# Output projection of a hybrid attention layer: two 16-bit halves instead of two four-byte halves, and its weights loaded earlier

## The chip, the cores and the metric

One core of one Trainium2 chip runs the whole layer as one program. The metric is the device time of one execution in microseconds; lower is better. Engines are named as in the profile: PE is TensorE (PEld its weight loads), DVE is VectorE, ACT is ScalarE, POOL is GpSimd, SP is SyncE, which issues nearly all DMAs here.

## The reference, cut to what matters

A layer takes 1024 prompt tokens and 8 x 8 sample tokens of width 1024, normalises them, projects them with one wide matrix into queries, keys, values and gates, runs two kinds of attention (a sparse one with a compressed, a selected and a window branch, 8 heads; and a dense one with forget gates, 8 heads, called fox), and merges:

```
def merge_out(x, oa, za, ob, zb, w_out):
    B, T, _ = x.shape
    u = jnp.concatenate([oa.reshape(B, T, -1) * jax.nn.silu(za), ob.reshape(B, T, -1) * jax.nn.silu(zb)], axis=-1)
    return x + jnp.einsum('btm,md->btd', u, w_out).astype(x.dtype)
```

`w_out` is 1024 x 1024 in four-byte floats (4.2 MB). The change concerns this last product, for the prompt (`yp`) and for the samples (`ys`).

## The kernel before, in words

Prompt tokens are worked on in 8 tiles of 128, the 64 sample tokens as a ninth (t = 8, `NT`). The kernel runs in stages that flow into one another.

1. Projections (about 0 to 520 us). Fifteen chunks of columns of the input matrix (`chunks`, L800), each for nine token tiles. Operands are split into a high and a low 16-bit half, and a product is three matmuls: high x high, high x low, low x high (`project`, L240). `load_w` (L181) loads a chunk, squares it on ScalarE for its norm, scales it by the norm and splits it. While chunk ci runs, at its fourth tile, the functions of `background` (L808) for that chunk are called: compression of cached tokens, masks, decay sums. Chunks 5 to 8 are the keys and queries of the fox heads. `x_tile` (L158) loads the tokens at the start into buffers `xin` (5 of them), with squares into `xsq`.
2. Fox attention (about 400 to 595 us), the last projection chunks woven in.
3. Sparse tiles 0 to 3 (L1421, about 580 to 775 us), the samples' attention woven in by `fill` (L954) from `sample_filler` (L1394). A tile (`nsa_tile`, L1378) loads and splits the next tile's keys and queries (L1004, L1018), takes row maxima on VectorE (`nsa_max`, L1036), and per pair of key blocks computes scores on TensorE, the exponential `pf` and its high half `phi` on ScalarE (L1103, L1104), the low half `plo` on VectorE or, in every third case here, on GpSimd (L1106), and three matmuls with the values (`pv`, L719).
4. Sparse tiles 4 to 7 (L1576) and the output projection (L1448 to L1579). Weights: `load_wout` (L1454) loads 128 rows in two halves of 512 columns into `wos` (2 buffers); ScalarE writes the high half `woh` (L1459), GpSimd the low half `wol` (L1460), both as F32R, a four-byte matmul format. `project_out` (L1462) does a tile: load `z` (the gates, parked in DRAM) and `obl` (the fox result), four VectorE products into `z` (L1475), eight transposes (L1485), `uh` on ScalarE (L1487), `ul` on VectorE (L1488), 2 x 24 matmuls of 512 columns (L1499), addition of the input token (L1501). `z`, `uh`, `ul` and `xr` have one buffer each. For the samples high and low halves lie side by side and 2 x 16 matmuls do (L238, called from L1495). `project_last` (L1523) does tile 7 in three parts (fox columns, then two pairs of blocks of the sparse result), accumulating all three into the same two PSUM banks, and adds the token at the end (L1552).

Order of work. The program is written as a sequence; a scheduler that simulates a timeline (L1609) then fixes the order of each engine's instructions ahead of the run, taking later work early where its operands and buffers are free. In the run each engine, and SyncE as issuer of DMAs, goes through its list in order. The output projections stand behind tiles 4 to 7 in the program and are pulled forward between their instructions. On-chip memory of the samples' pools (`S5`) is freed at L1446, and the pools of the output projection are laid there.

## Time and profile before

| what | value |
| --- | --- |
| median of 3 runs | 977.35 us (974.95 to 984.67) |
| profiled execution | 974.53 us |
| its span (first to last instruction) | 972.8 us |
| mean granted TensorE clock in it | 0.988 |
| TensorE busy | 901.1 us (93%) |
| VectorE / ScalarE / GpSimd busy | 644.9 / 612.3 / 397.4 us |
| DMA | 111.73 MB, mean 115 GB/s |

A matmul's duration in the trace (0.39 us for 512 columns) overlaps with its neighbours; the distance between starts is what a stream of them costs. "Busy" of an engine is the union of its instructions.

### The profile page before, as it was taken

To read this page: it belongs to the slowest core of one execution; us is meant where nothing else is said; L and a number is where in the kernel's file an instruction comes from. 1 tells how busy PE (TensorE), PEld (TensorE's weight loads), DVE (VectorE), ACT (ScalarE), POOL (GpSimd) and SP (SyncE) were. 2 spreads that over 40 slices of the span, in tenths; PEclk is the share of its full clock that TensorE was granted. 3 is DMA by queue.
4 is the path that set the end of the run, shared out by engine and by line. 5 is a ranking of instruction groups with operands and counts; after the bars stand their busy time and mean duration, and the time that the engine had idled before them with its cause. 6 is when DMAs were issued, how large, how long until landed. Compare 5 with 4: busy or idle time off the path is not lost.

```text
span 972.8 us, 24636 instructions
## 1 busy us (share of the span) xinstructions
PE 901.1 (93%) x9097; PEld 707.1 (73%) x9097; DVE 644.9 (66%) x1845; ACT 612.3 (63%) x1328; POOL 397.4 (41%) x571
## 2 busy tenths in 40 slices
PE   4898999889999999999998888889999979999997
PEld 3687889878888988878786556656666645776776
DVE  5764666564555426768777566887888989776552
ACT  6844643433454665797786779888897868454540
POOL 4544567754676432342425123434333157211100
PEclk9999999999999999999999899999999999999999
DMA  7563323422343332331314755555355032231241
GB/s 267 142 154 110 90 81 89 107 59 70 98 117 99 117 106 65 106 110 54 88 43 125 234 154 154 164 170 177 114 167 185 5 129 97 97 108 57 76 140 66
DMA packets 119740, 111.73 MB, mean 115 GB/s; under 512 B 37100, under 2 KB 100244, under 8 KB 119596
## 3 DMA queue, kind: packets, MB, share of 16 engines
q1 hardware_dynamic: 117732, 106.74, 36.4%
q0 software_dynamic: 1456, 2.83, 1.3%
q8 instruction: 71, 1.16, 0.5%
q10 hardware_dynamic: 432, 0.59, 0.2%
q14 instruction: 49, 0.40, 0.1%
HBM read 79.57 MB, written 27.41 MB: 110 GB/s over the span
## 4 chain that ended last, share of the span: by engine, by line
PE 64%; DVE 9%; DMA 7%; ACT 6%; issue 3%; POOL 2%; SPq 1%; DVEq 0%; ACTq 0%; POOLq 0%
PE acc L245 22%; PE ctr L1499 7%; PE sa L474 3%; PE acc L238 3%; PE smax L1054 2%; PE pv L726 2%; PE pv L724 2%; PE pv L725 2%; PE st L1098 2%; PE st L1099 2%; DMA wst<-in_w_in_dram 2%; DVE junk L744 2%; PE ctr L1547 1%; PE st L774 1%; PE st L775 1%
## 5 line engine op out<-in xcount | busy, mean ns | idle before, releaser
L245 PE MATMUL acc<-wsp,xth 128*128 128x256 f16 (+1 forms) x1920 | 334.7, 275 | 5.1 <-ACT xth L175 2.6
L245 PE MATMUL acc<-wsp,xtl 128*128 128x256 f16 (+1 forms) x960 | 264.1, 275 | 0.0
L245 PEld LDWEIGHTS <-xth 128*128 128x128 f16 x1920 | 187.3, 99 | 33.7 <-ACT xth L175 3.1
L1103 ACT ACTIVATE pf<-st,nsc 128x512 f32<-128x512 f32 x132 | 99.0, 780 | 49.6 <-PE st L1099 26.9
L245 PEld LDWEIGHTS <-xtl 128*128 128x128 f16 x960 | 94.5, 98 | 14.8 <-issue 1.4
L724 PEld LDWEIGHTS <-phi 128*128 128x128 f16 x816 | 76.9, 97 | 17.0 <-issue 5.5
L726 PEld LDWEIGHTS <-plo 128*128 128x128 f16 x816 | 76.7, 99 | 9.8 <-DVE plo L1106 2.4
L1104 ACT ACTIVATE phi<-pf 128x1024 f16<-128x1024 f32 (+1 forms) x76 | 71.7, 948 | 14.0 <-PE pv L726 8.8
L725 PEld LDWEIGHTS <-phi 128*128 128x128 f16 x816 | 76.8, 97 | 4.7 <-issue 1.5
L1106 DVE TENSOR_TENSOR plo<-pf,phi 128x1024 f16<-128x1024 f32 (+1 forms) x58 | 67.0, 1158 | 10.8 <-ACT phi L1104 10.0
L711 ACT ACTIVATE pf<-st,nsc 128x512 f32<-128x512 f32 (+1 forms) x96 | 62.5, 670 | 16.1 <-PE st L775 5.2
L264 POOL TENSOR_TENSOR nss<-nss,nhalf 128x4 f32<-128x4 f32 (+3 forms) x72 | 68.4, 950 | 4.4
L724 PE MATMUL pv<-va,phi 128*128 128x65 f16 x528 | 59.0, 193 | 4.3 <-DVE nt L1083 3.4
L716 DVE TENSOR_TENSOR plo<-pf,phi 128x512 f16<-128x512 f32 (+3 forms) x77 | 51.6, 674 | 16.0 <-ACT phi L714 15.7
L201 ACT ACTIVATE vsq<-wst 128x512 f16<-128x512 f32 (+2 forms) x72 | 40.2, 559 | 33.4 <-DMA wst<-in_w_in_dram 32.5
L725 PE MATMUL pv<-va,phi 128*128 128x64 f16 x528 | 58.9, 195 | 0.0
L726 PE MATMUL pv<-va,plo 128*128 128x65 f16 x528 | 56.4, 192 | 0.4 <-DVE plo L1106 0.2
L1106 POOL TENSOR_TENSOR plo<-pf,phi 128x1024 f16<-128x1024 f32 (+1 forms) x18 | 34.6, 1923 | 51.4 <-ACT phi L1104 40.6
L714 ACT ACTIVATE phi<-pf 128x512 f16<-128x512 f32 (+1 forms) x96 | 48.7, 524 | 10.3 <-PE pv L726 8.8
L1054 PE MATMUL smax<-kma,nqm 88*128 88x512 f16 (+3 forms) x192 | 49.1, 316 | 3.8 <-DVE nm L744 3.5
L1084 POOL TENSOR_TENSOR oa<-oa,nt 128x256 f32<-128x256 f32 x22 | 19.7, 894 | 78.8 <-DVE nt L1083 65.0
L1098 PE MATMUL st<-nqm,kma 88*128 88x512 f16 x132 | 50.2, 380 | 0.9 <-ACT pf L1103 0.7
(446 smaller groups left out, 2402.6 us busy)
## 6 DMA issues: line engine op xcount, KB each, us to landing
wst<-in_w_in_dram SPq DMA_DIRECT2D x56, 256.0 KB
sfk<-in_cache_fox_kv_dram SPq DMA_DIRECT2D x32, 256.0 KB
sfv<-in_cache_fox_kv_dram SPq DMA_DIRECT2D x32, 256.0 KB
out_dram<-kv SPq DMA_DIRECT2D x52, 128.0 KB
xin<-in_x_prompt_dram SPq DMA_DIRECT2D x8, 512.0 KB
cpair<-in_cache_nsa_cmp_kv_dram SPq DMA_DIRECT2D x64, 64.0 KB
zpark<-z SPq DMA_DIRECT2D x32, 128.0 KB
spg<-in_cache_nsa_slc_kv_dram SPq DMA_DIRECT2D x32, 128.0 KB
```

The costliest lines, as they stand in the source:

```text
L245: nc.tensor.matmul(ps[:, :n], x[:, k, t * 128:(t + 1) * 128], w[k // 2][:, i, k % 2, :n], start=(k == 0 and j == 0), stop=(k == KT - 1 and ...
L264: nc.gpsimd.tensor_tensor(ss[:n, 0, :h], ss[:n, 1, :h], nhalf[:n, :h], op=ALU.pow)
L711: nc.scalar.activation(p[:n, :cols], ps[:n, :cols], AF.Exp, bias=nsc[:n, 3:4], scale=nsc[:n, 6:7])
L724: nc.tensor.matmul(po[:, s, 0:65], hi[:, c], v[:, 0:65], start=f, stop=False, skip_group_check=True)
L725: nc.tensor.matmul(po[:, s, 0:64], hi[:, c], v[:, 65:129], start=False, stop=False, skip_group_check=True)
L726: nc.tensor.matmul(po[:, s, 0:65], lo[:, c], v[:, 0:65], start=False, stop=l, skip_group_check=True)
L1054: nc.tensor.matmul(pr[:, r], qm[0:88, (r0 + r) * 128:(r0 + r + 1) * 128], kma[0:88, 2 * k + g, j0 * 128:j1 * 128], start=r == 0, stop=not ...
L1098: nc.tensor.matmul(ps, kma[0:88, 2 * k + g, c], qm[0:88], start=True, stop=False)
L1103: nc.scalar.activation(pf[:, 512 * x:512 * x + 512], ps, AF.Exp, bias=nsc[:, 3:4], scale=nsc[:, 2:3])
L1104: nc.scalar.activation(hi[:, 0:n], pf[:, 0:n], AF.Copy)
L1106: (nc.gpsimd if turn[0] % share[mixed[0]] == 0 else nc.vector).tensor_sub(lo_[:, 0:n], pf[:, 0:n], hi[:, 0:n])
L1499: nc.tensor.matmul(ps, l[:, k], w[:, k, c], start=(k == 0 and j == 0), stop=(k == KT - 1 and j == 2))
```

## The change

Weights and tokens of the output projection are held as 16-bit halves. So that they fit the 16-bit range, the weights are scaled by one factor from the norm of the whole matrix, each token's row by a factor from its own norm, and the product is scaled back where the input token is added. The matrix's norm is computed during chunks 5 to 9 of the projections (`wout_squares`, `wout_scale`), which loads the matrix once more; the splitting load moves to the start of each of the sparse tiles 0 to 3, two blocks of rows per tile. In `project_last` each of the three parts gets its own scale and its own accumulation, added to `x` in turn; the last part uses the score banks.

```
+    wsc = P.tile([128, 16], F32, name="wsc")
...
+    def wout_squares(ks):
+        for k in ks:
+            s = B.tile([128, D], F32, name="xin", bufs=5)
+            nc.sync.dma_start(s, w_out[:, k])
+            junk = B.tile([128, D], F32, name="xsq")
+            nc.scalar.activation(junk, s, AF.Square, accum_out=wsc[:, k:k + 1])
+    def wout_scale():
+        p = PS.tile([128, 8], F32, name="sa", bufs=1)
+        nc.tensor.matmul(p, ones, wsc[:, 0:8], start=True, stop=True)
+        nc.vector.tensor_reduce(out=wsc[:, 10:11], in_=p, axis=AX.X, op=ALU.add)
+        nc.vector.tensor_scalar(wsc[:, 11:12], wsc[:, 10:11], 2.0 ** -30, TINY, op0=ALU.mult, op1=ALU.add)
+        nc.gpsimd.tensor_tensor(wsc[:, 8:9], wsc[:, 11:12], nhalf[:, 0:1], op=ALU.pow)
+        nc.vector.reciprocal(wsc[:, 9:10], wsc[:, 8:9])
...
-                  4: [lambda: cmp_cached(2)], 5: [lambda: cmp_cached(3)], 6: [sample_compressed, lambda: score_scales()],
-                  7: [setup_masks, finish_gates], 8: [fox_decay, load_logf], 9: [fox_first]}
+                  4: [lambda: cmp_cached(2)], 5: [lambda: cmp_cached(3), lambda: wout_squares((0, 1))],
+                  6: [sample_compressed, lambda: score_scales(), lambda: wout_squares((2, 3))],
+                  7: [setup_masks, finish_gates, lambda: wout_squares((4, 5))],
+                  8: [fox_decay, load_logf, lambda: wout_squares((6, 7))], 9: [fox_first, wout_scale]}
...
+    W3 = S3.enter_context(tc.tile_pool(name="wout", bufs=1, reuse_waits="tile"))
+    woh = W3.tile([128, KT, D], F16, name="woh")
+    wol = W3.tile([128, KT, D], F16, name="wol")
+    def load_wout(k):
+        for h in range(2):
+            c = slice(512 * h, 512 * h + 512)
+            st = W3.tile([128, 512], F32, name="wos", bufs=2)
+            nc.sync.dma_start(st, w_out[:, k, c])
+            nc.scalar.activation(st, st, AF.Copy, scale=wsc[:, 8:9])
+            nc.scalar.activation(woh[:, k, c], st, AF.Copy)
+            nc.gpsimd.tensor_sub(wol[:, k, c], st, woh[:, k, c])
     mixed[0] = 1
     for t in range(4):
+        for k in (2 * t, 2 * t + 1):
+            load_wout(k)
         qq = nsa_tile(t, qq)
...
+    def token_scale(u, n):
+        w = u.shape[-1]
+        junk = B6.tile([128, D], F16, name="uj", bufs=1)
+        s = B6.tile([128, 4], F32, name="us", bufs=4)
+        nc.scalar.activation(junk[:n, 0:w], u, AF.Square, accum_out=s[:n, 0:1])
+        nc.gpsimd.tensor_scalar(s[:n, 1:2], s[:n, 0:1], 2.0 ** -30, TINY, op0=ALU.mult, op1=ALU.add)
+        nc.gpsimd.tensor_tensor(s[:n, 2:3], s[:n, 1:2], nhalf[:n, 0:1], op=ALU.pow)
+        nc.scalar.activation(u, u, AF.Copy, scale=s[:n, 2:3])
+        nc.vector.reciprocal(s[:n, 3:4], s[:n, 2:3])
+        nc.vector.tensor_tensor(s[:n, 0:1], s[:n, 3:4], wsc[:n, 9:10], op=ALU.mult)
+        return s[:n, 0:1]
...
+        undo = token_scale(u[:n], n)
-        uh = B6.tile([128, KT, 128], F32R, name="uh", bufs=1)
+        uh = B6.tile([128, KT, 128], F16, name="uh", bufs=1)
...
-            nc.vector.tensor_tensor(x[:n, c], ps[:n], x[:n, c], op=ALU.add)
+            nc.vector.scalar_tensor_tensor(x[:n, c], ps[:n], undo, x[:n, c], op0=ALU.mult, op1=ALU.add)
...
+        for ks, src, early in ((slice(4, 8), obl, True), (slice(0, 2), nsa[:, 0:256], True), (slice(2, 4), nsa[:, 256:512], False)):
...
+            undo = token_scale(u, 128)
...
+                ps = PS.tile([128, 512], F32, name="ctr", bufs=CTR) if early else PM.tile([128, 512], F32, name="st", bufs=2)
...
+                nc.vector.scalar_tensor_tensor(x[:, c], ps, undo, x[:, c], op0=ALU.mult, op1=ALU.add)
+                if not early:
+                    nc.sync.dma_start(o["yp"][0, t * 128:(t + 1) * 128, c], x[:, c])
...
-    for k in range(KT):
-        load_wout(k)
```

## Rows read from the trace of the kernel before

**Rows 1.** The page, part 1: busy us, share of the span, instructions.
```profile
PE 901.1 (93%) x9097; PEld 707.1 (73%) x9097; DVE 644.9 (66%) x1845; ACT 612.3 (63%) x1328; POOL 397.4 (41%) x571
```

**Rows 2.** Busy time by stage: us, PE, PEld, DVE, ACT, POOL, PEclk, DMA share, GB/s.
```profile
0.00:60.00 60.00, 42.15 (x309) 34.87 (x310) 39.96 (x111) 41.88 (x114) 26.82 (x53) 0.97 0.67 203
60.00:400.00 340.00, 328.00 (x3011) 287.84 (x3009) 185.27 (x659) 168.21 (x447) 189.05 (x302) 1.00 0.34 95
...
580.00:775.00 195.00, 180.42 (x2292) 123.95 (x2292) 158.20 (x455) 166.55 (x335) 69.11 (x93) 0.99 0.49 148
775.00:820.00 45.00, 38.27 (x403) 23.86 (x402) 41.20 (x84) 32.31 (x48) 27.01 (x24) 1.00 0.32 105
820.00:955.00 135.00, 133.72 (x1114) 99.21 (x1113) 89.77 (x183) 65.04 (x89) 22.65 (x17) 1.00 0.28 93
955.00:973.00 18.00, 12.43 (x54) 9.34 (x52) 3.41 (x6) 1.36 (x3) 0.00 (x0) 1.00 0.24 87
```

**Rows 3.** Timeline of SP's queue from 740 us: start, us, issue.
```profile
783.15 0.33 SPq L1458 DMA_DIRECT2D wos<-in_w_out_dram  x1
...
797.29 26.60 SPq L1458 DMA_DIRECT2D wos<-in_w_out_dram  x10
```

**Rows 4.** Timeline of PE, 930 to 955 us: start, us, instruction.
```profile
930.74 0.47 PE L1499 MATMUL ctr<-wol,uh 128*128 128x512 f32 x1
931.05 0.39 PE L1499 MATMUL ctr<-woh,ul 128*128 128x512 f32 x1
...
933.18 0.38 PE L1098 MATMUL st<-nqm,kma 88*128 88x512 f16 x1
...
933.83 0.38 PE L1099 MATMUL st<-nq,k1a 128*128 128x512 f16 x1
...
949.15 0.39 PE L1499 MATMUL ctr<-woh,uh 128*128 128x512 f32 x1
...
954.36 0.40 PE L1499 MATMUL ctr<-woh,ul 128*128 128x512 f32 x1
```

**Rows 5.** Groups by line, 0 to 520 us: count, busy us, mean ns, idle before.
```profile
L217 POOL TENSOR_TENSOR wsp<-wst,wsp 128x512 f16<-128x512 f32 x36 | 42.5, 1192 | 10.7 <-ACT wsp L216 10.1
...
L215 ACT ACTIVATE wst<-wst,vst 128x512 f32<-128x512 f32 x36 | 23.6, 708 | 6.4 <-POOL vst L207 6.4
L216 ACT ACTIVATE wsp<-wst 128x512 f16<-128x512 f32 x36 | 21.5, 619 | 0.0
...
L162 ACT ACTIVATE xsq<-xin 128x1024 f32<-128x1024 f32 x8 | 8.4, 1055 | 1.4 <-DMA xin<-in_x_prompt_dram 1.4
...
L164 POOL TENSOR_TENSOR xst<-xst,nhalf 128x1 f32<-128x1 f32 x8 | 4.9, 610 | 0.5
```

**Rows 6.** Groups by line, 770 to 973 us: the weights' ScalarE copies.
```profile
L1459 ACT ACTIVATE woh<-wos 128x512 fp32r<-128x512 f32 x16 | 10.1, 630 | 5.9 <-DMA wos<-in_w_out_dram 5.9
```

**Rows 7.** Timeline at the end: VectorE's last gating products, TensorE's first transposes of tile 7.
```profile
948.40 0.88 DVE L1515 SCALAR_TENSOR_TENSOR z<-oa,zs,z 128x256 f32<-128x256 f32 x2
...
954.59 0.60 PE L1519 MATMUL ctr<-ident,z 128*128 128x128 f32 x4
```

**Rows 8.** The chain that ended last, 600 to 680 us: start, us, piece.
```profile
608.26 4.67 DMA sfv<-in_cache_fox_kv_dram
612.95 4.03 DMA kn<-out_dram
...
661.31 5.32 DMA sfv<-in_cache_fox_kv_dram
666.65 4.35 DMA kn<-out_dram
```

**Rows 9.** Timeline of VectorE and GpSimd, 930 to 955 us.
```profile
934.32 1.91 DVE L1084 TENSOR_TENSOR oa<-oa,nt 128x256 f32<-128x256 f32 x1
...
945.21 0.43 DVE L1084 TENSOR_TENSOR oa<-oa,nt 128x256 f32<-128x256 f32 x1
...
933.81 2.15 POOL L1106 TENSOR_TENSOR plo<-pf,phi 128x1024 f16<-128x1024 f32 x1 [10.78 <-PE st L1099]
```

More of the change, by code (lines that the diff above doesn't have):

```diff
@@ L1446, in layer_kernel @@
     S5.close()
-    W3 = ctx.enter_context(tc.tile_pool(name="wout", bufs=1, side="right", reuse_waits="tile"))
     B6 = ctx.enter_context(tc.tile_pool(name="outw", bufs=1, side="right", reuse_waits="tile"))
-    w_out = a["w_out"][0].rearrange("(kt p) n -> p kt n", p=128)
-    woh = W3.tile([128, KT, D], F32R, name="woh")
-    wol = W3.tile([128, KT, D], F32R, name="wol")
-    def load_wout(k):
-        for h in range(2):
-            c = slice(512 * h, 512 * h + 512)
-            st = B6.tile([128, 512], F32, name="wos", bufs=2)
-            nc.sync.dma_start(st, w_out[:, k, c])
-            nc.scalar.activation(woh[:, k, c], st, AF.Copy)
-            nc.gpsimd.tensor_sub(wol[:, k, c], st, f32(woh[:, k, c]))
+    def token_scale(u, n):
[9 more added lines that the diff above has]
+        return s[:n, 0:1]
     def project_out(t, oa):
@@ L1500, in project_out @@
                                          stop=(k == KT - 1 and j == 2))
[L1501 removed]
+            nc.vector.scalar_tensor_tensor(x[:n, c], ps[:n], undo, x[:n, c], op0=ALU.mult, op1=ALU.add)
             if t == NT:
[L1503 removed]
+                lo = B6.tile([64, 512], F32, name="ntl", bufs=1)
                 nc.scalar.activation(lo, ps[64:128], AF.Copy)
[L1505 removed]
+                nc.vector.scalar_tensor_tensor(x[:n, c], lo, undo, x[:n, c], op0=ALU.mult, op1=ALU.add)
@@ L1535, in project_last @@
-        uh = B6.tile([128, KT, 128], F32R, name="uh", bufs=1)
-        ul = uh[:, :, 64:128]
-        if t < NT:
-            ul = B6.tile([128, KT, 128], F32R, name="ul", bufs=1)
-        ps = [PS.tile([128, 512], F32, name="ctr", bufs=CTR) for _ in range(2)]
-        for ks, src in ((slice(4, 8), fox), (slice(0, 2), nsa[:, 0:256]), (slice(2, 4), nsa[:, 256:512])):
-            out_part(t, ks, src, z, uh, ul)
+        nc.sync.dma_start(x, xp[t * 128:(t + 1) * 128])
+        obl = B6.tile([128, 512], F32, name="obl", bufs=1)
@@ new lines, in project_last @@
+        nc.sync.dma_start(obl, obpark[t].rearrange("p h d -> p (h d)"))
+        nsa = flat(oa)
+        uh = B6.tile([128, KT, 128], F16, name="uh", bufs=1)
+        ul = B6.tile([128, KT, 128], F16, name="ul", bufs=1)
+        for ks, src, early in ((slice(4, 8), obl, True), (slice(0, 2), nsa[:, 0:256], True), (slice(2, 4), nsa[:, 256:512], False)):
+            m = ks.stop - ks.start
+            u = z[:, 128 * ks.start:128 * ks.stop]
+            for i in range(0, m, 2):
+                c = slice(128 * i, 128 * i + 256)
+                nc.vector.scalar_tensor_tensor(u[:, c], src[:, c], zs[:, (ks.start + i) // 2:(ks.start + i) // 2 + 1], u[:, c],
+                                               op0=ALU.mult, op1=ALU.mult)
+            undo = token_scale(u, 128)
+            p = PS.tile([128, 4, 128], F32, name="ctr", bufs=CTR)
+            for i in range(m):
+                nc.tensor.transpose(p[:, i], u[:, i * 128:(i + 1) * 128], ident)
+            nc.scalar.activation(uh[:, ks], p[:, 0:m], AF.Copy)
+            nc.vector.tensor_sub(ul[:, ks], p[:, 0:m], uh[:, ks])
@@ L1542, in project_last @@
             for h in range(2):
                 c = slice(512 * h, 512 * h + 512)
-                terms = ((uh, woh), (uh, wol)) if t == NT else ((uh, woh), (uh, wol), (ul, woh))
+                ps = PS.tile([128, 512], F32, name="ctr", bufs=CTR) if early else PM.tile([128, 512], F32, name="st", bufs=2)
                 for k in range(ks.start, ks.stop):
-                    for j, (l, w) in enumerate(terms):
-                        nc.tensor.matmul(ps[h], l[:, k], w[:, k, c], start=(k == 4 and j == 0),
-                                         stop=(k == 3 and j == len(terms) - 1), skip_group_check=True)
@@ L1549, in project_last @@
-            yield
-        for h in range(2):
-            c = slice(512 * h, 512 * h + 512)
-            nc.vector.tensor_tensor(x[:n, c], ps[h][:n], x[:n, c], op=ALU.add)
-            if t == NT:
-                lo = B6.tile([64, 512], F32, name="ntl", tag="wos", bufs=2)
-                nc.scalar.activation(lo, ps[h][64:128], AF.Copy)
-                nc.vector.tensor_tensor(x[:n, c], x[:n, c], lo, op=ALU.add)
-            nc.sync.dma_start(o["yp"][0, t * 128:(t + 1) * 128, c] if t < NT else o["ys"].rearrange("b t d -> (b t) d")[:, c],
-                              x[:n, c])
@@ L1560, in layer_kernel @@
-    for k in range(KT):
-        load_wout(k)
+                    for j, (l, w) in enumerate(((uh, woh), (uh, wol), (ul, woh))):
+                        nc.tensor.matmul(ps, l[:, k], w[:, k, c], start=(k == ks.start and j == 0),
+                                         stop=(k == ks.stop - 1 and j == 2))
+                nc.vector.scalar_tensor_tensor(x[:, c], ps, undo, x[:, c], op0=ALU.mult, op1=ALU.add)
+                if not early:
+                    nc.sync.dma_start(o["yp"][0, t * 128:(t + 1) * 128, c], x[:, c])
```

30 lines of the change are left out of this document (4 added, 26 removed).

## The prediction, made before the changed kernel was run

> **What bounds the kernel now.** I read the busy times first, then the same by stage, then the queue of SyncE, then single instructions. The reader is to see that TensorE is busy 901.1 of 972.8 us [rows 1], and that its idle rest is not spread evenly. By stage [rows 2] TensorE is busy 42.15 of 60 us at the start, 328.00 of 340 in the projections, 180.42 of 195 in the first four sparse tiles (580 to 775 us, with the sample work woven in), 38.27 of 45 in the stretch in which the output weights come in, 133.72 of 135 while output projection and sparse tiles 4 to 7 share the engine, and 12.43 of 18 in the tail. From 820 to 955 only less matmul time can help. From 775 to 820 there are 45 - 38.27 = 6.73 us of idle to be had. From 580 to 775 no engine is alone at its limit: TensorE 93%, ScalarE 166.55 of 195 (85%), VectorE 158.20 (81%); there added work can hurt.
>
> The weights arrive late: of 16 half loads SyncE issues the third at 783.15 us and the last ten over the 26.60 us from 797.29 [rows 3]. There are two staging buffers, each held through a DMA, a ScalarE copy and a GpSimd subtraction. The last load is out at 823.9 us, which is where the idle stretch ends.
>
> **The change part by part.** The sum is made against the profiled execution, 974.53 us, of which 972.8 is the span. That lies 2.82 us under the median of the three runs shown.
>
> *Matmuls.* The projection has 7 x 48 (tiles 0 to 6) + 2 x 16 (samples) + 48 (tile 7) = 416 matmuls of 512 columns. In the four-byte format 23 steps take 954.36 - 949.15 = 5.21 us, 0.2265 each. The 16-bit score matmuls of the same width take 0.65 us for three steps, 0.217 each [rows 4]. The difference of 0.0098 x 416 gives -4.1 us. A second, smaller part: where the four-byte stream resumes after short 16-bit matmuls, its first step is 931.05 - 930.74 = 0.31 us instead of 0.227, a loss of 0.08. The timeline has 58 such places after 770 us. Between nothing (the first step merely drains what stood before) and 58 x 0.08 = 4.8, I take -2. In this full stage matmul time is end time: -6.1, bounds 0 and -8.9.
>
> *Weights early.* The idle 6.73 us of 775 to 820 can go; some of it belongs to waits of the sparse tiles themselves, since VectorE is busy 41.20 of these 45 us [rows 2]. Beyond that the projection may begin before 775, where TensorE is idle 14.58 us over 195; the last quarter of that stretch gives up to another 3. Bounds 0 and -9.7; I take -5. What is late next is VectorE, which serves the sparse tiles' row maxima.
>
> *Token scale in the nine projections.* Per full tile ScalarE gets a square of 128x1024 (1.055 us) and a scaling of the same size, taken at the same duration; GpSimd gets two small operations of at most 0.610 us, VectorE two more [rows 5]. That is about 3.3 us between the gating products and the transposes. ScalarE has room: it is busy 32.31 + 65.04 of 180 us from 775 to 955 [rows 2] and loses 10.1 us of weight copies [rows 6]. TensorE is covered by the sparse tiles until about 945 us. After that the cover is tile 6's own matmuls: the gating of tile 7 is done at 948.40 + 0.88 = 949.3 us; square, two GpSimd operations and scaling of its first half (0.62 + 1.22 + 0.71) bring it to 951.8, and its transposes start only at 954.59 [rows 7]. So 2.8 us are to spare and I charge +1 for queueing. If that cover is gone, each of the last tile's three parts exposes 2.55 us: +7.7. The separate accumulations of tile 7 add four VectorE additions under matmuls.
>
> *Loads and splitting moved into 580 to 775.* Sixteen DMAs of 256 KB go onto SyncE's queue, among the page loads and the sparse tiles' key and query loads; 16 ScalarE scalings (0.708) and 16 copies (0.619), together 21.2 us; 16 GpSimd subtractions of 1.192, 19.1 us [rows 5], ahead of the transfers on GpSimd's queue that put keys and queries in place. GpSimd is free 126 us. ScalarE is free 28.45 us against 21.2 [rows 2]: it would stand at 96%. Each scaling waits for its own DMA, and behind it on ScalarE stand the exponentials, for which the score banks and so TensorE wait. Bounds: 0, all in the free time, and +21.2, none of it (not below 0, since nothing leaves this stage). I take +5, nearer to 0: the free time is scattered in waits on scores, where these copies fit; but the stage already has a page load and then a key load of together 8.70 and 9.67 us on the chain that sets the end [rows 8], and the same queue now gets 16 more transfers.
>
> *Norm of the weights.* Eight loads of 512 KB and eight squares of 1.055 us in the projection stage. ScalarE is busy 168.21 of 340 us there, so 8.4 us fit. The 4.2 MB are an estimated 21 us of DMA time at the 203 GB/s of the first 60 us. The queues are laid out in advance, and free buffers let these loads start early, perhaps into that first stage, where DMA is busy 0.67 [rows 2]. A square that waits for its load holds up ScalarE's evacuations behind it, and then TensorE. Bounds: 0 and +16, four pairs each late by the smallest wait of [rows 8], 4.03. I take +2, near 0, since TensorE is at 96% there although weight loads run all through it. The scale itself is five small operations, long before its first use.
>
> Sum: 974.53 - 6.1 - 5 + 1 + 5 + 2 = 971.4. The profiled execution lies 0.42 us below the fastest run shown, so for a median I add half a microsecond: **972 us**.
>
> A row that speaks against the moved GpSimd work: VectorE's addition in on-chip memory takes 1.91 us when it starts inside a 2.15 us GpSimd subtraction, ending 0.3 us after it, and 0.43 us otherwise [rows 9]. The Trainium skill, "SBUF — State Buffer", section "SBUF: two separate sides", says why: the two engines share a port pair as an exclusive lock, and a VectorE operation with two inputs there is fully blocked while GpSimd reads. The trace agrees with it; the time by it is rival D.
>
> **The rivals.**
>
> *A, all hidden.* ScalarE's free 28.45 us take the 21.2, the squares cost nothing, the idle 6.73 goes. At best 974.53 - 8.9 - 9.7 = 955.9; with the middle of the two gains, -6.1 and -7, 961.4. For it: no engine passes 96%. Against it: queues are in order, and VectorE is near its limit from 775 on.
>
> *B, ScalarE becomes the bound of 580 to 775* (the other side). Its 28.45 us of idle are waits for scores and loads which the new copies do not fill, because each waits in order for its own DMA and the exponentials stand behind it. Price: the full 21.2 us with the other terms kept, 974.53 - 6.1 - 5 + 1 + 21.2 + 2 = 987.6, slower by 1.3%. The other terms leave 966.4, so it decides the sign from 8.1 of the 21.2 us exposed and passes 1% (984.3) from 17.9. For it: 85% before, and the DMA waits of [rows 8]. Against it: TensorE is the stage's fullest engine.
>
> *C, the format gives nothing.* If three steps of [rows 4] are no measure of a long stream, the -6.1 falls away: 977.5. Within 1%.
>
> *D, GpSimd holds VectorE.* The 16 subtractions block VectorE in 580 to 775 for up to 16 x 1.192 = 19.1 us; they no longer do so from 781 to 827, where VectorE was just as full, so I price half: 971.4 + 9.5 = 981. For it: the rows named; against it: VectorE has 37 us free in that stage.
>
> **How the numbers follow.** Forecast 0.38, A 0.27, B 0.17, C 0.13, D 0.05. About 1% is what a measurement of this kernel can tell from no change. Faster by over 1% means A, and a sliver of the forecast: 0.28. Slower by over 1% means B, and the square loads at their upper end: 0.17. Same: 0.55. The range goes from A's middle less 3.4 to just above B: 958 to 988.
>
> **What would show it.** Right, if the projection's matmuls step at 0.217 us; if no weight load is issued after 775 us and TensorE's idle there falls below 3 us; if from 580 to 775 ScalarE rises to some 187 us busy and that stage grows by about 5 us; if the projection stage grows by about 2; if the tail keeps 17 to 18 us. Wrong, if the first 60 us grow with the squares' loads on the chain, if the sparse stage grows by over 15 us with ScalarE at its limit, or if the matmul steps stay at 0.227.

## The result and the profile after

The changed kernel takes 985.89 us (median of 20 runs, 980.99 to 991.87), the kernel before 977.97 (20 runs beside them, 974.04 to 984.67). The ratio is 1.0077, with a 95% interval of 1.0059 to 1.0096: slower by 0.8%. The forecast was 972. The profiled execution has a span of 984.3 us, 11.5 more than before.

Part 1 of the changed kernel's page, to be held against [rows 1]:

```profile
PE 903.6 (92%) x9099; PEld 678.4 (69%) x9099; DVE 650.8 (66%) x1874; ACT 650.9 (66%) x1393; POOL 402.4 (41%) x594
```

TensorE is busy 2.5 us longer although its stream got cheaper. The columns of the stages are those of [rows 2] (us, then busy PE, PEld, DVE, ACT, POOL, then granted clock, DMA share, GB/s):

```profile
0.00:60.00 60.00, 42.55 (x306) 35.04 (x307) 39.89 (x111) 44.08 (x118) 26.78 (x53) 0.97 0.67 208
60.00:400.00 340.00, 324.62 (x2916) 283.22 (x2915) 178.18 (x647) 165.85 (x438) 187.80 (x301) 0.98 0.36 103
580.00:775.00 195.00, 170.73 (x2106) 116.00 (x2107) 154.67 (x429) 169.71 (x339) 86.02 (x107) 0.97 0.52 157
775.00:820.00 45.00, 42.48 (x550) 27.48 (x549) 41.83 (x108) 38.26 (x67) 12.96 (x15) 1.00 0.24 77
820.00:955.00 135.00, 133.00 (x1167) 75.68 (x1166) 95.58 (x210) 84.97 (x116) 22.34 (x29) 0.99 0.26 81
955.00:985.00 30.00, 23.13 (x118) 10.63 (x115) 12.85 (x29) 5.57 (x14) 2.18 (x6) 0.98 0.30 105
```

The stretch from 775 to 820 idles 45 - 42.48 = 2.52 us instead of 6.73: that step of the prediction came true, and the last of the 16 weight loads is issued at 695.0 us. But the projections and the first sparse tiles hold less TensorE work in the same time, and the granted clock is below [rows 2] in both.

The matmul step, from TensorE's timeline in tile 6's projection (start, us, instruction):

```profile
962.80 0.38 PE L1538 MATMUL ctr<-woh,ul 128*128 128x512 f16 x1
...
965.61 0.38 PE L1538 MATMUL ctr<-woh,uh 128*128 128x512 f16 x1
```

Thirteen steps in 2.81 us (only the first and the last are shown) are 0.216 each, as forecast (0.217).

Where did the time come from? A span is the sum of three things that the trace gives: time without any TensorE instruction (idle), the part of its busy time that the lower clock adds (granted clock 0.5, the level of 1.2 GHz; half of the busy time spent there), and the rest, which is work at 2.4 GHz.

| profiled execution, us | span | idle | lower clock adds | rest |
| --- | --- | --- | --- | --- |
| before | 972.8 | 71.6 | 9.7 | 891.4 |
| changed | 984.3 | 80.7 | 16.8 | 886.8 |

The work fell by 4.6 us. Idle rose by 9.1, and the lower clock takes 7.1 more, a term that the prediction did not have at all. The Trainium skill, "TensorE: Matmul & The Clock Gate", section "Terms", prices the lower clock by the time there times one minus the ratio; the table does that for TensorE's busy time alone, and takes every number from the trace.

By milestones, the 577th matmul of the prompt's projections (three chunks of 192 are then through, at 129.9 us before; called "the third chunk" below) starts 8.9 us later than before, the first sparse tile's first exponential 10.9 us later, and the end is 11.5 us later. So most of the loss is there by 130 us, long before the code that the change is about. SyncE's queue in the changed kernel shows why to look there (L807 is the norm's load):

```profile
50.78 0.35 SPq L807 DMA_DIRECT2D xin<-in_w_out_dram  x1
51.25 0.36 SPq L322 DMA_DIRECT2D out_dram<-kv  x1
51.65 0.43 SPq L807 DMA_DIRECT2D xin<-in_w_out_dram  x1
52.18 1.08 SPq L434 DMA_DIRECT2D cw<-in_w_cmp_k_dram  x2
53.30 5.91 SPq L434 DMA_DIRECT2D cw<-in_w_cmp_v_dram  x2
59.31 2.53 SPq L494 DMA_DIRECT2D cpair<-out_dram  x2
61.89 1.58 SPq L807 DMA_DIRECT2D xin<-in_w_out_dram  x2
...
68.94 0.34 SPq L807 DMA_DIRECT2D xin<-in_w_out_dram  x1
```

All eight loads, written for chunks 5 to 8 (some 215 to 305 us), leave between 50.78 and 69 us. Their buffers `xin` come free as the token tiles are done (the last of `x_tile`'s GpSimd operations starts at 49.8 us), and the scheduler took the loads at once. The squares follow on ScalarE from 54.8 to 80.0 us. In the windows of that stretch TensorE loses first its work and then its clock:

```profile
60.00:75.00 15.00, 12.86 (x109) 10.87 (x108) 7.74 (x34) 8.42 (x19) 6.35 (x15) 0.92 1.04 328
75.00:79.00 4.00, 2.26 (x14) 1.41 (x13) 2.77 (x7) 4.00 (x13) 3.60 (x4) 0.86 0.55 129
79.00:90.00 11.00, 11.00 (x86) 9.66 (x85) 4.84 (x20) 7.15 (x25) 4.28 (x10) 0.84 0.60 168
```

From 60 to 75 us it is idle 2.14 us with the DMA engines full (share 1.04), from 75 to 79 us 1.74 us while ScalarE is busy throughout; from 79 to 90 it is busy throughout, but at a mean clock of 0.84.

### The profile page after: what moved, and what is told of

The parts are those of the page before. It is cut to its first block, busy times and chain, and to the rows that moved or that the text cites. A ratio compares the mean times of both kernels' runs of the same rounds, so it can differ in the third digit from the quotient of the medians.

```text
span 984.3 us, 24765 instructions
## 1 busy us (share of the span) xinstructions
PE 903.6 (92%) x9099; PEld 678.4 (69%) x9099; DVE 650.8 (66%) x1874; ACT 650.9 (66%) x1393; POOL 402.4 (41%) x594
## 4 chain that ended last, share of the span: by engine, by line
PE 51%; DVE 11%; DMA 10%; ACT 6%; POOL 5%; issue 4%; SPq 2%; DVEq 0%; POOLq 0%; ACTq 0%
PE acc L246 15%; PE ctr L1538 7%; DMA wst<-in_w_in_dram 2%; PE st L1120 2%; PE st L1121 2%; PE smax L1076 2%; PE pv L726 2%; PE pv L725 2%; PE pv L727 2%; POOL nss L265 2%; PE sa L475 2%; PE acc L239 1%; DMA nq<-qpark 1%; DVE junk L745 1%; DMA sfk<-in_cache_fox_kv_dram 1%
## 5 line engine op out<-in xcount | busy, mean ns | idle before, releaser
L246 PE MATMUL acc<-wsp,xth 128*128 128x256 f16 (+1 forms) x1920 | 338.7, 277 | 9.5 <-DVE va L308 2.5
L1128 DVE TENSOR_TENSOR plo<-pf,phi 128x1024 f16<-128x1024 f32 (+1 forms) x58 | 63.7, 1101 | 8.9 <-ACT phi L1126 8.7
L745 DVE CUSTOM_DVE_ANT_0 junk<-smax,maskw,nm 128x512 bf16<-128x512 f32 x64 | 47.7, 746 | 6.7 <-PE smax L1076 4.8
L1121 PE MATMUL st<-nq,k1a 128*128 128x512 f16 x132 | 50.7, 384 | 0.0
```

Source lines behind the costliest of these rows:

```text
L246: nc.tensor.matmul(ps[:, :n], x[:, k, t * 128:(t + 1) * 128], w[k // 2][:, i, k % 2, :n], start=(k == 0 and j == 0), stop=(k == KT - 1 and ...
L1121: nc.tensor.matmul(ps, k1a[:, 2 * k + g, c], q1, start=False, stop=not (diag or far))
L1128: (nc.gpsimd if turn[0] % share[mixed[0]] == 0 else nc.vector).tensor_sub(lo_[:, 0:n], pf[:, 0:n], hi[:, 0:n])
```

## The experiments

Each run is timed against the kernel before on the same chip. Clock is the median granted TensorE clock over the run's executions; for the kernel before it is 0.986 or 0.987 beside e1 to e18. Runs from different chips are compared by their ratios. By the intervals in the table the difference of two ratios is uncertain by some 0.003 to 0.005 (3 to 5 us, more for e2, e3 and e8); ranges behind such differences below are worked out from these intervals.

| run | what it is | us, median | before | ratio, 95% interval | clock |
| --- | --- | --- | --- | --- | --- |
| changed | the change | 985.89 | 977.97 | 1.0077, 1.0059 to 1.0096 | 0.980 |
| e1 | norm loads held to their chunks ("gated") | 977.83 | 975.98 | 1.0014, 0.9978 to 1.0050 | 0.981 |
| e2 | weight DMAs early, splitting late | 992.82 | 975.98 | 1.0157, 1.0094 to 1.0220 | 0.974 |
| e3 | loading and splitting late | 992.01 | 975.98 | 1.0137, 1.0076 to 1.0198 | 0.976 |
| e4 | splitting early, no weight DMAs | 984.09 | 975.98 | 1.0083, 1.0050 to 1.0117 | 0.981 |
| e5 | no norm | 982.54 | 977.15 | 1.0040, 1.0010 to 1.0070 | 0.978 |
| e6 | no norm, no token scale, late | 976.46 | 977.15 | 0.9992, 0.9966 to 1.0018 | 0.984 |
| e7 | no norm, no token scale, early | 978.66 | 977.15 | 1.0021, 0.9982 to 1.0060 | 0.982 |
| e8 | gated, scaling pass on GpSimd | 996.79 | 977.15 | 1.0213, 1.0153 to 1.0274 | 0.971 |
| e9 | gated, splitting without GpSimd | 982.55 | 976.35 | 1.0059, 1.0026 to 1.0093 | 0.979 |
| e10 | gated, late | 978.26 | 976.35 | 1.0017, 0.9997 to 1.0036 | 0.984 |
| e11 | gated, no token scale | 982.96 | 976.35 | 1.0071, 1.0041 to 1.0101 | 0.976 |
| e12 | gated, four staging buffers | 978.58 | 976.35 | 1.0018, 0.9988 to 1.0048 | 0.982 |
| e13 | norm loads alone | 981.17 | 976.24 | 1.0039, 1.0017 to 1.0060 | 0.980 |
| e14 | norm squares alone | 980.38 | 976.24 | 1.0043, 1.0025 to 1.0062 | 0.980 |
| e15 | e6 without the scaling pass | 969.54 | 976.24 | 0.9921, 0.9895 to 0.9947 | 0.988 |
| e16 | gated, late, splitting without GpSimd | 975.39 | 976.24 | 0.9978, 0.9957 to 0.9999 | 0.984 |
| e17 | weights unscaled, late | 969.62 | 975.87 | 0.9931, 0.9902 to 0.9960 | 0.984 |
| e18 | weights unscaled, early | 975.24 | 975.87 | 0.9984, 0.9958 to 1.0009 | 0.980 |

**The norm of the weights: e1, e3, e10, e5, e13, e14.** e1 makes the norm's loads wait until the next chunk's scale is there:

```
             s = B.tile([128, D], F32, name="xin", bufs=5)
+            nc.vector.tensor_copy(s[:, 0:1], loaded[2][:, 0:1])
             nc.sync.dma_start(s, w_out[:, k])
```

> The eight norm loads are held back: one VectorE copy from the scale of the next chunk writes each buffer first, so a load can be issued only in the chunk it was written for (about 200 to 310 us) and not at 51 to 69 us. Theory 1 (the loads, pulled forward past the compression's weights and page loads, cost the 7.7 us): the projections start as before, time falls by 6 to 8 us from the changed kernel's 986 to 978 to 980. Rival (the squares' ScalarE work and DMA traffic cost the same wherever they stand): no gain, 984 to 987.

The loads now leave from 215.9 to 302.5 us, the third chunk is 2.2 us late instead of 8.9, and the ratio falls from 1.0077 to 1.0014. That is 6 us (2 to 10). The same edit on the kernel with the late weights (e3 to e10, below) takes 1.0137 to 1.0017, 12 us (6 to 18). TensorE's windows from 60 to 130 us, first in the kernel before, then in the changed kernel, then in e1:

```profile
60.00:130.00 70.00, 66.60 (x580) 58.10 (x578) 40.58 (x161) 36.04 (x117) 37.43 (x74) 1.00 0.38 102
```

```profile
60.00:130.00 70.00, 63.51 (x506) 53.18 (x505) 36.93 (x146) 40.84 (x120) 35.79 (x70) 0.93 0.51 149
```

```profile
60.00:130.00 70.00, 66.46 (x564) 57.94 (x563) 39.18 (x153) 36.04 (x116) 35.84 (x71) 0.98 0.38 101
```

e5 leaves the norm out altogether:

```
-                  4: [lambda: cmp_cached(2)], 5: [lambda: cmp_cached(3), lambda: wout_squares((0, 1))],
+                  4: [lambda: cmp_cached(2)], 5: [lambda: cmp_cached(3)],
...
     def wout_scale():
+        nc.vector.memset(wsc[:, 8:9], 1024.0)
+        nc.vector.memset(wsc[:, 9:10], 2.0 ** -10)
```

> The norm of the weights is left out altogether (no loads of the matrix during the projections, no squares, no scale from them): the weights are scaled by the constant 1024 instead, so the output is that of another scale. All else as in the changed kernel. Theory (the pulled-forward loads of the norm cost 7 to 9 us, in TensorE's idle and in time at the lower clock, and nothing later): third chunk within 2 us of the kernel before instead of 8.9 later, time 7 to 10 us under the changed kernel, about 977. Rival (the gated run gained by another order of the sparse stage, not by the loads): third chunk back, but the time stays at 982 to 986, because the sparse stage grows as it did.

The third chunk was 4.5 us late, more than either said, and the time was 982.54, the rival's figure. By ratio that is 0.0026 above e1, although this kernel does less, but within the two intervals. So the norm's price by this pair is 0.0077 - 0.0040 of 976 us, 3.6 us (0 to 7), and by the gates 6 and 12 us. Each edit also changes the static order of all that follows, so a price from one pair holds to some 5 us at best; e11, below, does less than e1 and takes longer.

e13 and e14 part the loads from the squares. In e13 nothing reads the loaded rows:

```
             junk = B.tile([128, D], F32, name="xsq")
-            nc.scalar.activation(junk, s, AF.Square, accum_out=wsc[:, k:k + 1])
```

> The changed kernel with the norm's eight loads in their early place and nothing that reads them: squares and scale are left out, the weights are scaled by the constant 1024. Theory (the transfers cost: they go ahead of the compression weights and share the DMA engines with the projection's own weights): third chunk 7 to 9 us later than in the kernel before, and the time as the changed kernel's, 983 to 986. Rival (the squares cost, which stand on ScalarE ahead of the evacuations): third chunk within 3 us, time as without the norm, 978 to 982.

In e14 the squares read a constant tile:

```
-            nc.sync.dma_start(s, w_out[:, k])
...
-            nc.scalar.activation(junk, s, AF.Square, accum_out=wsc[:, k:k + 1])
+            nc.scalar.activation(junk, wz, AF.Square, accum_out=wsc[:, k:k + 1])
```

> The changed kernel without the norm's loads; its eight squares stay in their early place on ScalarE but read a constant tile, and the weights are scaled by the constant 1024. Theory (the transfers cost): third chunk within 3 us of the kernel before, time 978 to 982. Rival (the squares cost, 8 x 1.06 us on ScalarE between 55 and 80 us): third chunk 6 us or more later, time 983 to 986.

The third chunk is 3.2 us late with the loads alone and 6.4 with the squares alone; both together make 8.9, and 9.5, 11.0 and 9.5 in e2, e3 and e4, which have the same loads. But in the thirteen kernels without early norm work the third chunk comes anywhere from 0.8 us earlier to 4.5 us later than before (e5 is the latest of them). So the early norm as a whole is clear of all of them, 8.9 to 11.0 us in four kernels, and the squares alone are above them; the loads alone are not told from none. In total time e13 and e14 are alike, 1.0039 and 1.0043, and so is e5 with neither, 1.0040: neither part alone shows a cost there, and both together take 3.6 us more. How the two share the loss stays open. The windows from 60 to 130 us, of e13 and then of e14:

```profile
60.00:130.00 70.00, 65.61 (x559) 56.67 (x557) 38.83 (x150) 35.64 (x111) 34.96 (x70) 0.98 0.54 157
```

```profile
60.00:130.00 70.00, 64.98 (x535) 55.98 (x533) 35.93 (x148) 39.99 (x122) 36.36 (x71) 0.95 0.38 101
```

**What the early weights cost, and what: e2, e4, e3, e10, e12.** e2 holds the whole matrix in sixteen staging buffers; the splitting waits until the samples' memory is free.

```
-            st = W3.tile([128, 512], F32, name="wos", bufs=2)
-            nc.sync.dma_start(st, w_out[:, k, c])
+            staged[k, h] = W4.tile([128, 512], F32, name="wos", bufs=16)
+            nc.sync.dma_start(staged[k, h], w_out[:, k, c])
```

> Only the 16 DMAs of the weights stay in sparse tiles 0 to 3 (sixteen staging buffers); scaling, copies and subtractions are held until the samples' memory is free, after about 780 us. Theory ACT (the 21.2 us of ScalarE work fills the stage): the sparse stage gives back 8 to 11 us, the last stage loses 3 to 5, so 980 to 983 in all. Theory DMA (16 more transfers in front of key, query and page loads on SyncE's queue): the stage keeps its 11 us, the last stage loses 3 to 5, so 988 to 991.

e4 splits a constant tile in place of the weights:

```
-            nc.sync.dma_start(st, w_out[:, k, c])
-            nc.scalar.activation(st, st, AF.Copy, scale=wsc[:, 8:9])
+            nc.scalar.activation(st, wz, AF.Copy, scale=wsc[:, 8:9])
```

> The 16 weight DMAs are left out: the scaling reads a constant tile, so the weights are not the layer's and the output product is not computed from them; the 32 ScalarE operations and 16 GpSimd subtractions stay in sparse tiles 0 to 3. Theory ACT: the sparse stage keeps at least 8 of its 11 us, 983 to 986. Theory DMA: it falls back by 8 to 11 us, 975 to 978.

Without the DMAs the time stays (1.0083 against 1.0077), as theory ACT said: the sixteen transfers in the sparse stage cost nothing that shows. e2, at 992.82, is above both theories. Without the splitting, e2 gives the sparse stage most of its growth back: from its first exponential to the compressed branch's of tile 5 it takes 180.0 us with 13.6 idle, against 177.8 with 12.8 before, 186.1 with 21.2 in the changed kernel and 185.1 with 21.0 in e4. But the sixteen splittings in one lump then stop TensorE, and its clock falls. e2 from 780 us:

```profile
780.00:800.00 20.00, 18.49 (x219) 11.11 (x218) 18.86 (x49) 17.07 (x30) 5.08 (x5) 1.00 0.19 68
800.00:818.00 18.00, 10.21 (x103) 7.63 (x104) 13.91 (x25) 12.79 (x22) 18.00 (x16) 0.53 0.06 15
818.00:830.00 12.00, 8.73 (x90) 4.20 (x87) 11.69 (x27) 8.62 (x12) 9.88 (x11) 0.91 0.09 18
```

In the 18 us in which GpSimd is busy throughout, TensorE is busy 10.21 us at a granted clock of 0.53.

e3 puts `load_wout` back behind the samples, with its three operations; e10 is e3 with the gate of e1.

```
     for t in range(4):
-        for k in (2 * t, 2 * t + 1):
-            load_wout(k)
         qq = nsa_tile(t, qq)
...
+    for k in range(KT):
+        load_wout(k)
     done.append((NT, None))
```

> Loading and splitting of the weights moved back behind the samples, on memory that their pools free, as in the kernel before; 16-bit halves, norms and token scales stay. If the move cost 11 us in the sparse stage and gained 5 in the last one, this takes 6 us off: 979 to 981, of which 7.7 us over the kernel before are the norm's loads. If the sparse stage grew for another reason (the later start of the samples), no more than 2 us come off.

> The whole computation. The gated run with loading and splitting of the weights put back behind the samples, as in the kernel before. Against the gated run it measures the early weights with the first stage undisturbed; against the run with the late weights it measures the gate. Theory (late load loses about 6 us by TensorE's idle and the lower clock after it): 984. Rival (with the format alone the late load cost nothing, so early and late are worth the same): 976 to 979.

e3 was the slower way, and e10 came out as the rival said. With the norm's loads held back, early (e1, 1.0014) and late (e10, 1.0017) are worth the same. That agreed with the prediction's -5 and +5, but both carry the scaling pass and the norm. Against the kernels without these (e17 late, e18 early, below) they cost 0.0086 in the late place, 8.4 us (5 to 12), and 0.0030 in the early one, 2.9 us, which is not told from zero.

e12 gives the staging tile four buffers instead of two:

> The whole computation. The gated run with four staging buffers for the weights instead of two, so that a load is issued two halves ahead. Theory (ScalarE stands 8.3 us in the gated run waiting for a staged half to land, with the exponentials queued behind it): 2 to 5 us under the gated run, 973 to 976. Rival (the passes on ScalarE and GpSimd themselves cost, and their DMAs nothing, as in the run without the DMAs): as the gated run, 977 to 979.

The rival's outcome: 978.58, against 977.83 for e1, although ScalarE's waits for staged halves fell from 8.3 to 3.2 us. They were not what the stage pays for.

**Other engines for the splitting: e8, e9.** e8 has two buffers for `xr` besides.

```
-            nc.scalar.activation(st, st, AF.Copy, scale=wsc[:, 8:9])
+            nc.gpsimd.tensor_scalar(st, st, wsc[:, 8:9], None, op0=ALU.mult)
```

> The whole computation, three edits to the changed kernel: the norm's loads held to their chunks as in the gated run; the scaling of the weights on GpSimd instead of ScalarE (16 operations of 128x512, 11.3 us of ScalarE less in the sparse stage); two buffers for the input token's tile, so that the load for tile 7 doesn't wait for the output of tile 6. Theory (ScalarE's queue is what the splitting costs): 3 to 5 us under the gated run's 978 by the splitting and 1 by the buffer, about 972 to 974, below the kernel before. Rival D of the prediction (GpSimd's operations hold VectorE): at or above the gated run, 977 to 982.

Worse than the rival said, by 19 us against e1. The groups by line of e8's GpSimd, from 580 to 810 us:

```profile
L1452 POOL TENSOR_SCALAR wos<-wos,wsc 128x512 f32<-128x512 f32 x16 | 27.5, 1721 | 16.8 <-DMA wos<-in_w_out_dram 11.1 <-DVE nl L1099 5.4
```

One scaling takes 1.721 us there, against 0.731 on ScalarE in the changed kernel (first line below; the three passes of the splitting, same columns):

```profile
L1451 ACT ACTIVATE wos<-wos,wsc 128x512 f32<-128x512 f32 x16 | 11.7, 731 | 5.0 <-DMA wos<-in_w_out_dram 4.9
L1452 ACT ACTIVATE woh<-wos 128x512 f16<-128x512 f32 x16 | 10.2, 644 | 0.0
...
L1453 POOL TENSOR_TENSOR wol<-wos,woh 128x512 f16<-128x512 f32 x16 | 19.6, 1228 | 4.0 <-ACT woh L1452 3.9
```

e9 drops the scaling pass and GpSimd's subtraction:

```
-            nc.scalar.activation(st, st, AF.Copy, scale=wsc[:, 8:9])
-            nc.scalar.activation(woh[:, k, c], st, AF.Copy)
-            nc.gpsimd.tensor_sub(wol[:, k, c], st, woh[:, k, c])
+            nc.scalar.activation(woh[:, k, c], st, AF.Copy, scale=wsc[:, 8:9])
+            nc.vector.scalar_tensor_tensor(wol[:, k, c], st, wsc[:, 8:9], woh[:, k, c], op0=ALU.mult, op1=ALU.subtract)
```

> The whole computation. Against the gated run, the splitting in the sparse stage changes engines: the high half is one ScalarE copy with the scale in it, the low half one VectorE operation (staged times scale minus high half); the scaling pass of ScalarE (16 x 0.73 us) and the 16 GpSimd subtractions (16 x 1.17 us) are gone. Theory (the stage pays for GpSimd's slow two-input operations and for ScalarE's extra passes, since the run that put a third pass on GpSimd grew by 19 us): 5 to 8 us under the gated run, 970 to 973 where the kernel before is at 977. Rival (VectorE, at 81% of that stage before, becomes the bound): 16 x 0.7 = 11 us more on VectorE, the time at or above the gated run, 978 to 985.

982.55, the rival's outcome: with 12.0 us more on VectorE, 10 less on ScalarE and 19 less on GpSimd it is not faster than e1. That it is slower is not shown: 0.0045 by ratio, with 0.0049 of uncertainty.

**Format, scaling pass, token scale: e6, e7, e11, e15, e17, e18, e16.** The first three leave the token scale out; e7 is e5 with this edit, e6 besides loads late as e3 does, and e11 is e1 with it.

```
     def token_scale(u, n):
-        w = u.shape[-1]
...
-        return s[:n, 0:1]
+        return wsc[:n, 9:10]
```

> Left out: the norm of the weights (constant 1024 instead) and the scale of each token's row (constant 1); loading and splitting of the weights stand behind the samples as in the kernel before. What is left of the change is the 16-bit format, one ScalarE scaling more per half load, and tile 7 in three accumulations. Theory (format worth 416 steps of 0.0098 us and some resumptions): 6 us under the kernel before, so 970 to 973 where that is at 977. Rival C of the prediction (format gives nothing to the time): within 1.5 us of the kernel before. A third way, from the run with the late weights: the weight load behind the samples costs more than before, because TensorE runs dry there and the granted clock falls; then the time is above the kernel before by 2 us or more.

> Left out: the norm of the weights (constant 1024) and the scale of each token's row (constant 1). The weights are loaded and split during the sparse tiles 0 to 3 as in the changed kernel. Against the run without the norm it measures the token scale: forecast term +1 us, so 976; rival (the three parts of the last tile each expose 2.55 us, +7.7): 7 us under that run, 970. Against the run with the format alone it measures the early weights: by the prediction 0 us in sum (-5 of gain, +5 of cost); if the splitting costs the sparse stage the 8 us that the runs without it gave back, and the late load the 8 us that they lost, also 0.

> The gated run without the scale of each token's row (constant 1 in its place; the output is the same up to rounding in the low halves). It measures the token scale by itself: the prediction's term is +1 us, so 976.5 to 977.5 here; its upper bound of 7.7 us would give 970.

e6 came out like rival C, within 1 us of before. But C's reason is wrong: the work at full clock fell by 5.0 us (886.4 against 891.4), and idle (+3.3) and the lower clock (+1.3) took it back. e7 is 2.2 us above e6 and 3.9 under e5, neither of which is told from zero by the ratios. e11, by neither expectation, is slower than e1 without the token scale, 5.6 us by ratio (1 to 10); its trace has 1.7 us less idle than e1's, and 8.9 us more that the lower clock adds. The token scale costs nothing that can be told from this.

What took e6's gain? In its late load, SyncE issues the last twelve half loads (start, us, issue):

```profile
797.66 39.52 SPq L1476 DMA_DIRECT2D wos<-in_w_out_dram  x12
```

The last is out at 837.2 us, against 823.9 before [rows 3]: each staging buffer is now held through three passes instead of two. e15 is e6 with the scaling pass removed; the weights are split unscaled, and the product is still multiplied by 1/1024 at the end. e17 multiplies by 1 and keeps the token scale; e18 is e17 with the weights early.

```
             nc.sync.dma_start(st, w_out[:, k, c])
-            nc.scalar.activation(st, st, AF.Copy, scale=wsc[:, 8:9])
             nc.scalar.activation(woh[:, k, c], st, AF.Copy)
```

> The run with the format alone (no norm, no token scale, late weights), and besides without the scaling pass over the staged weights, which are split unscaled. Theory (that pass, 16 x 0.73 us on ScalarE in the late load, lengthens TensorE's idle there and takes the format's gain back): 3 to 5 us under the run with the format alone, 971 to 973 where the kernel before is at 976.5. Rival (the gain goes into idle elsewhere, or into the lower granted clock): within 1.5 us of that run, 975 to 977.

> No norm of the weights and no scale for them (they are split as they are, so their low halves keep fewer bits); token scale kept; loading and splitting behind the samples with the two operations of the kernel before. Theory (the added scaling pass in the late load took the format's gain back; the token scale costs about 1 us): 970 to 973 where the kernel before is at 976, ratio 0.994 to 0.997. Rival (the run without the pass gained by leaving the token scale out): 976 or more.

> As the run with unscaled weights, but loaded and split during the sparse tiles 0 to 3. Theory (early and late place are worth the same, as the gated pair showed with three operations; with two the early place loses less): 970 to 974. Rival (the early place lowers the granted clock whatever the splitting, through more short idle stretches in the sparse stage): 977 to 981.

Here the gain is. e15 is 6.9 us below e6 (3 to 10) by one pass of 16 x 0.73 us. The way from the pass to the time is only in part in the traces: from 775 to 850 us TensorE is idle 6.7 us in e15 and 9.0 in e6. e17, which is e15 with the token scale and another constant, is at 0.9931: 6.3 us under the kernel before, the fastest version of this study that keeps the projection's meaning, at the price of fewer bits in the low halves. The pair e15 and e17 is the closest measure of the token scale, 1.0 us (-3 to 5). e17's last loads, from the same view as above:

```profile
797.61 2.94 SPq L1476 DMA_DIRECT2D wos<-in_w_out_dram  x2
803.85 16.01 SPq L1476 DMA_DIRECT2D wos<-in_w_out_dram  x7
```

They are out at 819.9 us. e15's are out only at 826.6, in the same total time, so the moment of the last load alone doesn't give the gain. e17's page, part 1, has the cheaper stream at last, 890.9 us busy against 901.1 before [rows 1]:

```profile
PE 890.9 (92%) x9097; PEld 673.2 (70%) x9097; DVE 650.1 (67%) x1873; ACT 632.3 (66%) x1361; POOL 403.4 (42%) x593
```

e18, early, is 5.6 us slower than e17 on the same chip, a little under the rival's figure: the early place does cost once nothing else is in the way. Its windows by stage, after those of e17:

```profile
595.00:775.00 180.00, 164.68 (x2102) 112.03 (x2095) 149.98 (x432) 150.76 (x299) 62.74 (x83) 1.00 0.48 145
775.00:820.00 45.00, 39.40 (x407) 24.24 (x406) 40.85 (x86) 37.53 (x56) 30.00 (x30) 0.92 0.34 105
```

```profile
595.00:775.00 180.00, 162.10 (x1992) 109.24 (x1989) 145.36 (x413) 154.27 (x313) 83.56 (x103) 0.98 0.54 167
775.00:820.00 45.00, 43.10 (x438) 25.52 (x436) 38.57 (x93) 30.47 (x44) 9.29 (x13) 1.00 0.23 76
```

From 775 to 820 e18 has 3.7 us more of TensorE work, as the prediction wanted. From 595 to 775 it has 2.6 less, and at a lower clock. In the profiled pair idle is equal (74.2 and 73.9 us) and the lower clock takes 15.8 against 7.8 us. More than half of that, 9.8 against 4.9, falls before the first sparse exponential, where both kernels do the same. From there on e18 has 28.2 us of idle against 27.5 and 6.0 at the lower clock against 2.9. So in this pair it is the clock that the early place costs, with little more idle; that is one execution of each. Over the twelve executions of each the median clocks are 0.980 and 0.984.

e16 keeps the whole computation: gate, late load, and e9's two-operation splitting, now behind the samples.

> The whole computation: norm loads held to their chunks, token scale kept, weights loaded behind the samples, and split there by one ScalarE copy with the scale and one VectorE operation instead of two ScalarE passes and a GpSimd subtraction. Theory (the late load is bound by the time that a staging buffer is held): TensorE's idle between 775 and 850 us shrinks by 3 to 5 us against the same run with the three passes, time 973 to 975. Rival (VectorE, busy 41.20 of the 45 us from 775 to 820 in the kernel before, becomes the bound): 980 or more.

975.39, ratio 0.9978 (0.9957 to 0.9999): with the norm and the scale kept, faster than before by 0.2%, barely told from no change, 1% under the change as it was made, and 3.8 us under e10 (1 to 7). Its last load is out at 802.64 + 21.45 = 824.1 us. Its idle from 775 to 850 did not shrink, though, as the theory had it: TensorE is busy 65.93 of these 75 us, against 66.06 in e10. So where this run gains is not shown.

## Why the prediction was wrong

The sign was wrong: -5.4 us of the median shown was forecast, +7.9 measured. The time lies inside the stated range, and the change within the 1% called "same", but not for the reasons given: three terms of the sum missed.

The profiled pair can be held against the sum by stretches. Up to the first sparse exponential +2 was forecast (the norm), and 10.9 us were lost. From there to the compressed branch's exponential of tile 5 (773.6 us before) +5 was forecast (loads and splitting), and 8.2 were lost. For the rest -10.1 was forecast (-6.1, -5 and +1), and 7.6 were gained.

By ratios to the kernel before, the parts line up as a path over e17, e18 and e1 to the changed kernel, and each step can be held against its terms.

- *Format and token scale* (before to e17, late load): forecast -6.1 + 1 = -5.1, measured -6.7 (interval -9.6 to -3.9). Right, and for the reason given: the median step is 0.216 us in e17 too, 0.227 before, and TensorE's work at full clock falls from 891.4 to 883.1 us. The cover for the last tile's scaling held, too: from the last sparse result to the end it takes 984.3 - 958.1 = 26.2 us in the changed kernel, against 972.8 - 945.6 = 27.2 before. (The "at most 0.610 us" for a small GpSimd operation is the mean of its group, whose longest took 1.010; nothing hung on it, as the like operation takes 0.551 on average in the changed kernel.)
- *Early place* (e17 to e18): forecast "I take -5" and "I take +5", together 0; measured 0.9984 - 0.9931, 5.2 us lost (1 to 9). The gain from 775 to 820 is there (idle 2.52 us in the changed kernel). The cost of the stage before was the mis-sized term: 8.2 us in the profiled pair instead of 5. The bound was ScalarE's free time, and the prediction looked there for the limit (rival B). But ScalarE was not full: 169.71 of 195 us, not 187, and 166.8 of the 186.1 us of the sparse stretch itself (90%). In that stretch the changed kernel loses 8.4 us to TensorE's idle and 1.7 to the lower clock; in e18, which splits in two operations, idle there is only 0.8 us above e17's, and the lower clock takes 3.4 us where e17 has none. e4 shows that the transfers are no part of it that can be told, e12 that the wait for them isn't either.
- *Scaling pass and the norm at its written place* (e18 to e1): 1.0014 - 0.9984, 2.9 us (-1 to 7, so not told from zero), which the forecast had inside the terms above.
- *Norm taken early* (e1 to the changed kernel): forecast "I take +2, near 0, since TensorE is at 96% there although weight loads run all through it"; measured 6.2 us by this pair (2 to 10), 12 by the late pair (6 to 18), 3.6 by leaving it out (0 to 7). This is the step that failed most plainly: the third chunk is 8.9 to 11.0 us late in the four kernels with the early norm, and at most 4.5 in the thirteen without. The mechanism was in the text, loads pulled into the first stage by free buffers with a bound of +16. The value was taken as if they would be spread over the stage, and the squares as if ScalarE's mean share decided. They went in one lump at 50 to 80 us, behind a stage in which DMA was already busy 0.67 [rows 2], and TensorE lost 3.1 us of idle and 5.0 at the lower clock between 60 and 130 us.

Since each step starts where the last one ends, their sum, -6.7 + 5.2 + 2.9 + 6.2 = +7.6, is the measured ratio again and no check. The second thing missing is the clock: every saving or cost was priced at full clock, and the changed kernel's profiled execution spends 7.1 of its 11.5 us on the lower one.

Rival B named the right side for a part of the loss, but with the wrong engine as bound. Rival D is small in the traces. VectorE's operations of the sparse stage (595 to 790 us) that start while GpSimd works take together 17.8 us more in the changed kernel than the medians of the same operations at other times, but 13.5 before: 4 us more of VectorE's time by this estimate, not the 9.5 of end time that D asked. e8, slower by 19 us than e1 with more GpSimd work there, has 13.7 (to 810 us) against 10.4 in e1, so VectorE being held explains little of it; what does, GpSimd's own queue or another, is not shown.

What stays open: how much of the early place's 5 us is the order that the scheduler happened to choose, why the granted clock is lower with it, and why e11 is slower than e1.

The last tile got a new wait, too. `xr` has one buffer, so its load for tile 7 (issued at 969.90 us) follows tile 6's output (967.24), and VectorE's timeline shows the first addition behind it:

```profile
973.27 1.41 DVE L1578 SCALAR_TENSOR_TENSOR xr<-ctr,us,xr 128x512 f32<-128x512 f32 x2 [5.06 <-DMA xr<-in_x_prompt_dram]
```

TensorE then waits 0.96 us for a bank. No run changes this buffer alone.

## What to carry to other kernels

When a scheduler lays the queues out ahead, a load whose buffer is free is issued as early as the buffer allows and not where the code stands: price it where it will land, in one lump, or make its buffer depend on something late. Count the passes over each staged half where two buffers hold up the loads: one added pass of 0.73 us per half cost 7 us (3 to 10) in the late place and took the format's gain back. Where TensorE bounds a kernel, read the granted clock by stage beside the busy time: the lower clock took nearly as much of the loss as idle did, and not in proportion to it (the sparse stretch of e4 has 21.0 us of idle and nothing at the lower clock, that of e5 18.7 and 8.4). And a difference of two kernels smaller than their intervals is no price.

## What the runs showed of the hardware

- Executions of one kernel differ with the granted clock. In the 25 executions of the kernel before that stand beside e5 to e8 it runs from 0.979 to 0.993, and a straight line through them gives 7.2 us for 0.010 and accounts for 68% of the variance; in the 26 beside e13 to e16 it accounts for only 6%. All variants but e15 had a median clock below that of the kernel before, and the two slowest had the lowest: 0.971 (e8) and 0.974 (e2).
- A scaling of 128x512 four-byte values took 1.721 us on GpSimd and 0.731 on ScalarE; a copy to 16 bits on ScalarE took 0.722 with a scale from memory (e9) and 0.630 without (e18).
